# Moving the projections to the first half of the recurrent chain, and the long convolution beside its second half

## The chip, the cores and the metric

The kernel runs on one core of one Trainium2 chip. The metric is the device time of one execution in microseconds (us); the time before is the median of three runs.

## The reference

The model has two layers over 1024 latent tokens and 256 context tokens of width 1024. A layer normalises its tokens and multiplies them with one input projection, whose columns feed four groups of heads; each group's output is gated, the four are concatenated, multiplied with an output projection and added to the stream:

```
h   = rms_norm(x) * (1 + scale) + shift
z   = h @ w_in                     # 29 blocks of 128 columns
A   = hyena(z_hy)                  # two long two-sided convolutions, via a DFT
B   = rwkv7(z_rw)                  # both directions, a chain over blocks of 128 tokens
C   = window_attention(z_wa)       # +-128 tokens, context, a sink
D   = dense_attention(z_fa)        # all tokens and context
x   = x + gate * (concat(A,B,C,D * silu gates) @ w_out)
```

Layer 0 works on latent and context tokens, layer 1 (the last) needs only the latent output.

## The kernel before, in words

The program is written as straight code; a scheduler places every instruction on its engine by a simulated time line. Code that stands earlier has precedence, and work that stands later fills the gaps as far as its data and its memory are there. Memory comes from pools, and each pool lies on one of two sides of SBUF, as on a stack: the left side (the default) or the right side (`tc.using_default_side(R)`). A pool that is opened after another was closed on the same side takes its place, and each of its tiles waits until the tiles that lay there are done.

`program` goes through these stages in each layer:

- The normalised input as two operands (`hhi` and `hlo`, 80 KB a partition, left side) and `Proj` on top of it (left). `rw` makes the recurrent columns, two gate blocks follow (`PACE['pre']`), then `attn` makes queries, keys and values.
- `Rwkv.phase_a` (right side): `stage_a` for ten blocks of 128 tokens, and `solve` after the fourth, the eighth and the tenth. The last TensorE work of a block writes the bank `p_r` (L618).
- `Rwkv.phase_b` (right side, in the place of phase A): `stage_b` for ten blocks, each followed by the chain of states (`p_ch`); after the last one the blocks that one direction had left open (`pend`) follow.
- `w.beside`: the twelve projection blocks that are left (six gate blocks, six of hyena), 24 matmuls for each of three token groups in layer 0 and of two in layer 1, all at L245. Their weights are split by ScalarE (L231) and by GpSimd (`wl`, L232). They have no order of their own: `K.mark` notes the last TensorE instruction of every block of phase A (weight 1.3) and B (1.0, the first one 4.5) and of the seven late `pend` steps (0.5), 30 in all, and `K.spread` gives each token group a point between the shares `f0` and `f1` of that sum. Its matmuls are then queued behind the last mark at or before the point (`issue_after`). Phase A reaches to 13/30 = 0.433 of the sum. 
- Then all of `Proj` and the operands are closed on the left. `hyena` (for the latent tokens) and, in layer 0, `ctx_hyena` (for the context) have their pools on the right side, in the place of phase B. `attention` has its pools on the left side, in the place of the operands: window attention first (a = 0), then dense attention (a = 1), ten blocks of 128 queries each in layer 0 and eight in layer 1; each block ends with one GpSimd instruction at L1028. `OutProj` lies on the right; in layer 0 its normalised tiles are written into operands for layer 1 on the left, which are opened after attention is closed.

In hyena a half of the channels goes through `forward` twice and `inverse` twice; `forward` loads the filter's spectrum `Kf` (L1391), and its sums of eight (`Dft.eight`, `odd`, `even`) and products run on VectorE and GpSimd beside each other. SyncE (SP) issues nearly all DMAs, in order.

The functions and lines that the text speaks of:

Of the kernel before, what the change touches and what calls it, by code (L numbers as in the profile page):

```python
# [12 lines left out]
PSUM = bass.MemoryType.PSUM  # L13
# [7 lines left out]
EPS = 1e-6  # L21
B_HY, B_HYG, B_RW, B_RWG, B_WA, B_WAG, B_FA, B_FAG = 0, 6, 8, 15, 17, 21, 23, 27
NBLK = 29
PACE = {'pre': (2, 2), 'w0': (0.0, 0.0), 'wt': (3.5, 3.5), 'f0': (0.3, 0.3), 'f1': (0.7, 0.7)}


def consts():
# [126 lines left out]
def operands(hp):  # L154
    return [hp.tile([128, 8, TOK], F32R, name=n) for n in ("hhi", "hlo")]
# [265 lines left out]
class Rwkv:  # L421
# [22 lines left out]
    def phase_a(w, ep, sp, pp):  # L444
# [30 lines left out]
        def stage_a(b, n):  # L475
# [138 lines left out]
            for d in range(2):  # L614
                for h in range(4):
                    for c in range(2):
                        z = half(1 - c)
                        nc.tensor.matmul(pr[half(c), d, h, :], GA[z, d, h % 2, h // 2, c, :], VS[z, h * 64:h * 64 + 64], start=True, stop=True)  # L618
            k.mark(1.3 + (PACE["w0"][l] if n == 0 else 0.0))
            cpy(AL[:, 1], pr.rearrange("p d h v -> p d (h v)"))  # L620
# [38 lines left out]
    def phase_b(w, sp, pp):  # L659
# [28 lines left out]
        def stage_b(b, n):  # L688
# [86 lines left out]
            if need_y:  # L775
# [5 lines left out]
                cpy(ST[:, 1536:1792].rearrange("p (h v) -> p h v", h=4), py)  # L781
            k.mark(1.0 + (PACE["wt"][l] if n == 0 else 0.0))
            return ST
# [286 lines left out]
class OutProj:  # L1070
# [24 lines left out]
    def bank(w, nm):  # L1095
        return w.pp.tile([128, 512], F32, tag="o", bufs=3, name=nm)
# [263 lines left out]
def hyena(k, l, kd, sp, pp):  # L1360
# [3 lines left out]
    n, p, R = L, 128, R8  # L1364
    bank = lambda nm: pp.tile([128, 512], F32, tag="b", bufs=3, name=nm)
    tile_ = lambda shape, tag, bufs=1, P=128: sp.tile([128] + shape, F32, tag=tag, bufs=bufs, name=tag)[:P]
# [20 lines left out]

    def forward(o_, hf):
        u = U[hf]
        Kf = tile_([R, 2, 128], "Kf", 2, p)  # L1390
        nc.sync.dma_start(out=Kf, in_=kd[o_, hf])  # L1391

        def tr(rs):
            ps = bank("pr").rearrange("p (r j e) -> p r j e", r=2, j=2)[:p]
            for a, r in enumerate(rs):
                for j in range(2):
                    nc.tensor.matmul(ps[:, a, j], F[:, r, j, :], u[:, r, :], start=True, stop=True)
            return ps

        W = tile_([R, 2, 128], "W", 2, p)  # L1400
        S, D = ft.tl(4, "s4"), ft.tl(4, "s4")
        ft.pair(S[:, 2:4], D[:, 2:4], tr((1, 3)), tr((5, 7)))
        ft.pair(S[:, 0:2], D[:, 0:2], tr((0, 2)), tr((4, 6)))
        ft.eight(W, S, D, False)
        t = tile_([R, 2, 128], "t", 1, p)
        h = R // 2
        for a, z, e in ((h, R, TT), (0, h, PT)):
            s = slice(a, z)
            e(t[:, s], W[:, s], Kf[:, s, 1:2, :].to_broadcast([p, z - a, 2, 128]), op=ALU.mult)
            e(W[:, s], W[:, s], Kf[:, s, 0:1, :].to_broadcast([p, z - a, 2, 128]), op=ALU.mult)  # L1410
            e(W[:, s, 0], W[:, s, 0], t[:, s, 1], op=ALU.subtract)
            e(W[:, s, 1], W[:, s, 1], t[:, s, 0], op=ALU.add)
        Z = tile_([R, 2, 128], "Z", 2, p)
        S, D = ft.tl(4, "s4"), ft.tl(4, "s4")
        TT(D[:, 2:4], W[:, 4:6], W[:, 6:8], op=ALU.subtract)
        TT(D[:, 0:2], W[:, 0:4:2], W[:, 1:4:2], op=ALU.subtract)
        PT(S[:, 0:2], W[:, 0:4:2], W[:, 1:4:2], op=ALU.add)
        PT(S[:, 2:4], W[:, 4:6], W[:, 6:8], op=ALU.add)
        ft.eight(Z, S, D, True)
        return Z  # L1420
# [32 lines left out]
    for o_ in range(2):  # L1453
        Zs = []
        for hf in range(2):
            Zs.append(forward(o_, hf))
            yield
        for hf in range(2):
            inverse(o_, hf, Zs[hf])
            yield  # L1460
# [112 lines left out]
def program(nc, tc, A, out):  # L1573
    k = K(nc, tc, A)
    hyenas = (("", hy_filters, hyena, [2, 2, 128, R8, 2, 128]), ("c", ctx_filters, ctx_hyena, [2, 128, 2, 2, 256]))
    run = lambda g: [None for _ in g]
    R = "right"
    with k.pool("cp", 1) as cp, k.pool("dp", 1, DRAM) as dp:
        setup(k, cp, dp)

        def filters(l):
            for nm, f, _, shape in hyenas[:2 if l < DEPTH - 1 else 1]:
                k.kd[l, nm] = dp.tile(shape, F32, name=f"kd{l}{nm}")
                with tc.using_default_side(R), k.pool(f"hf{l}{nm}") as sp, k.pool(f"hfp{l}{nm}", 1, PSUM) as pp:
                    run(f(k, l, k.kd[l, nm], sp, pp))

        k.kd = {}
        for l in range(DEPTH):
            last = l == DEPTH - 1
            rw = Rwkv(k, l, cp, dp)  # L1590
            with ExitStack() as es:
                if l == 0:
                    held = ExitStack()
                    with tc.using_default_side(R):
                        ap = es.enter_context(k.pool("raw"))
                    hi, lo = norm_in(k, held.enter_context(k.pool(f"hp{l}")), ap)
                filters(l)
            with held:
                with k.pool(f"pj{l}") as sp, k.pool(f"pjp{l}", 1, PSUM) as pp:
                    w = Proj(k, l, hi, lo, sp, pp)  # L1600
                    run(w.rw())
                    todo = [(g, i) for g in (1, 2, 3, "h", 0) for i in range(6 if g == "h" else 2)]
                    early = PACE["pre"][l]
                    w.beside(todo[:early])
                    if not last:
                        for a, parts in ((l, (1,)), (l + 1, (0, 1))):
                            with tc.using_default_side(R), k.pool(f"mod{a}") as rs, k.pool(f"modp{a}", 1, PSUM) as rp:
                                modulation(k, a, parts, 3, rs, rp)
                    with k.pool(f"pa{l}") as sa, k.pool(f"pap{l}", 1, PSUM) as pq:
                        run(w.attn(sa, pq))  # L1610
                    with tc.using_default_side(R), k.pool(f"re{l}") as re, k.pool(f"ra{l}") as rs, k.pool(f"rap{l}", 1, PSUM) as rp:
                        run(rw.phase_a(re, rs, rp))
                    with tc.using_default_side(R), k.pool(f"rb{l}") as rs, k.pool(f"rbp{l}", 1, PSUM) as rp:
                        run(rw.phase_b(rs, rp))
                    w.beside(todo[early:], PACE["f0"][l], PACE["f1"][l])
                k.marks = []
            with ExitStack() as es:
                at = ExitStack()
                for nm, _, f, _ in hyenas[:1 if last else 2]:
                    with tc.using_default_side(R), k.pool(f"hy{l}{nm}") as rs, k.pool(f"hyp{l}{nm}", 1, PSUM) as rp:  # L1620
                        run(f(k, l, k.kd[l, nm], rs, rp))
                sp, pp = at.enter_context(k.pool(f"at{l}")), at.enter_context(k.pool(f"atp{l}", 1, PSUM))
                with tc.using_default_side(R):
                    op = OutProj(k, l, es.enter_context(k.pool(f"op{l}")), es.enter_context(k.pool(f"opp{l}", 1, PSUM)))
                for a in range(2):
                    run(attention(k, l, a, sp, pp))
                at.close()
                if last:
                    op.tiles(range(8), out)
                else:  # L1630
                    held = ExitStack()
                    hi, lo = operands(held.enter_context(k.pool(f"hp{l + 1}")))
                    with k.pool(f"nrmp{l}", 1, PSUM) as pp:
                        op.tiles([8, 9] + list(range(8)), out, (hi, lo, pp))
# [26 lines left out]
```

## Time and profile before

| | us |
|---|---|
| median of three runs | 2611.66 (2608.37 to 2614.43) |
| the profiled execution | 2599.59 |
| its span | 2597.8 |
| TensorE matmul busy | 2294.4 (88% of the span) |
| VectorE busy | 1696.6 (65%) |
| ScalarE busy | 1105.8 (43%) |
| GpSimd busy | 1012.8 (39%) |
| granted TensorE clock, mean | 0.913 |

Busy shares are means over the span. Matmuls are pipelined and their ends are modelled, so that a busy TensorE is not TensorE at its peak. The granted clock is a share of 2.4 GHz, 0.5 being 1.2 GHz.

### The profile page before, as it was taken

How to read it: one execution, taken by the hardware profiler on the slowest of the kernel's cores; microseconds unless marked ns; L12 is line 12 of the kernel's file. 1: busy time of each engine (PE TensorE's matmuls, PEld its weight loads, DVE VectorE, ACT ScalarE, POOL GpSimd, SP SyncE). 2: the span in 40 equal slices, each digit the busy share in tenths (PEclk: the TensorE clock that was granted, in tenths of full speed). 3: DMA queues.
4: the chain of work that ended last, by engine and by line, in shares of the span. 5: the costliest groups of instructions: out<-in, count | busy, mean ns of one | idle time of the engine just before them, and what ended most of it. 6: DMA issues, size and time to landing. Idle time of an engine off the chain costs nothing. (4 is left out here: it accounts for less than half of the span.)

```text
span 2597.8 us, 45285 instructions
## 1 busy us (share of the span) xinstructions
PE 2294.4 (88%) x16864; PEld 1873.1 (72%) x16864; DVE 1696.6 (65%) x3669; ACT 1105.8 (43%) x2622; POOL 1012.8 (39%) x1279
## 2 busy tenths in 40 slices
PE   7799999889999898878897997998999979887698
PEld 3688678667788786656686887976777868666466
DVE  6985247698734567797344776677886345779933
ACT  5422224444232576545444221344443347654451
POOL 1631223366622114464322233324676211336542
PEclk9899998779999899889998998987799989998799
DMA  7223773544364746411444124335445475641152
GB/s 261 93 90 112 247 219 116 151 143 147 107 228 141 196 150 159 165 33 70 139 129 133 72 74 152 114 112 147 136 133 161 161 201 171 163 154 49 42 162 98
DMA packets 288696, 359.12 MB, mean 138 GB/s; under 512 B 108007, under 2 KB 229910, under 8 KB 283100
## 3 DMA queue, kind: packets, MB, share of 16 engines
q1 hardware_dynamic: 264008, 271.04, 33.6%
q0 software_dynamic: 11232, 70.78, 7.9%
q10 hardware_dynamic: 13236, 14.40, 2.0%
q8 instruction: 133, 2.18, 0.3%
q14 instruction: 87, 0.71, 0.1%
HBM read 227.31 MB, written 128.84 MB: 137 GB/s over the span
## 5 line engine op out<-in xcount | busy, mean ns | idle before, releaser
L232 POOL TENSOR_TENSOR wl<-wr,wh 128x1024 fp32r<-128x1024 f32 x58 | 145.1, 2507 | 276.2 <-ACT wh L231 198.9
L986 DVE TENSOR_REDUCE st<-S 128x1 f32<-128x512 f32 (+1 forms) x320 | 173.2, 557 | 102.0 <-PE S L982 57.7
L245 PE MATMUL acc<-hhi,wh 128*128 128x512 f32 (+1 forms) x896 | 222.8, 387 | 15.0 <-ACT wh L231 10.0
L981 PE MATMUL S<-kp,qs 128*128 128x256 f32 (+2 forms) x384 | 151.0, 402 | 85.5 <-ACT P L996 64.1
L245 PE MATMUL acc<-hlo,wh 128*128 128x512 f32 (+1 forms) x896 | 215.8, 376 | 2.6 <-DVE hlo L211 2.6
L996 ACT ACTIVATE P<-S,st 128x512 f32<-128x512 f32 (+1 forms) x320 | 184.2, 588 | 79.4 <-DVE st L989 74.2
L245 PE MATMUL acc<-hhi,wl 128*128 128x512 f32 (+1 forms) x896 | 216.0, 376 | 0.0
L245 PEld LDWEIGHTS acc<-hhi,wh 128*128 128x128 f32 x896 | 160.8, 198 | 50.4 <-ACT wh L231 11.9
L1012 PE MATMUL pt<-ident,P 128*128 128x128 f32 x976 | 169.0, 296 | 29.8 <-ACT PT L952 23.3
L245 PEld LDWEIGHTS acc<-hlo,wh 128*128 128x128 f32 x896 | 157.8, 193 | 33.5 <-DVE hlo L211 3.1
L952 ACT COPY PT<-pt 128x512 f32<-128x512 f32 (+2 forms) x298 | 141.0, 497 | 88.0 <-PE pt L1012 86.2
L245 PEld LDWEIGHTS acc<-hhi,wl 128*128 128x128 f32 x896 | 155.1, 191 | 31.7 <-issue 3.2
L1012 PEld LDWEIGHTS pt<-ident,P 128*128 128x128 f32 x976 | 122.1, 150 | 61.6 <-ACT PT L952 30.7
L981 PEld LDWEIGHTS S<-kp,qs 128*128 128x128 f32 x384 | 78.5, 205 | 114.9 <-ACT P L996 78.0
L1022 PE MATMUL O<-PT,V 128*64 128x256 f32 x976 | 132.1, 388 | 3.3 <-ACT PT L952 2.7
L982 PE MATMUL S<-kp,qs 128*128 128x256 f32 (+2 forms) x384 | 126.7, 342 | 3.7 <-DMA kp<-qk_d 3.7
L1022 PEld LDWEIGHTS O<-PT,V 128*64 128x64 f32 x976 | 70.6, 138 | 45.6 <-issue 6.7
L340 ACT ACTIVATE qx<-acc 128x256 f32<-128x256 f32 x76 | 29.2, 385 | 171.6 <-PE acc L335 152.5
L231 ACT ACTIVATE wh<-wr 128x1024 fp32r<-128x1024 f32 x58 | 60.7, 1057 | 94.3 <-PE acc L245 75.0
L589 PEld LDWEIGHTS p_g<-AR,BKT 64*128 64x128 f32 x640 | 77.0, 221 | 30.9 <-issue 6.8
L335 PE MATMUL acc<-wh,hhi 128*128 128x256 f32 x608 | 95.0, 298 | 4.5 <-ACT qx L340 2.5
L335 PE MATMUL acc<-wl,hhi 128*128 128x256 f32 x608 | 92.4, 290 | 6.4 <-POOL wl L232 6.4
(404 smaller groups left out, 5918.7 us busy)
## 6 DMA issues: line engine op xcount, KB each, us to landing
IN<-in_d POOLq DMA_DIRECT2D x18, 2048.0 KB, 9.4
wr<-in_w_in POOLq DMA_DIRECT2D x58, 512.0 KB, 4.6
mw<-in_mod_w SPq DMA_DIRECT2D x48, 512.0 KB
in_d<-BK SPq DMA_DIRECT2D x20, 512.0 KB
in_d<-AL SPq DMA_DIRECT2D x20, 512.0 KB
kp<-qk_d SPq DMA_DIRECT2D x32, 320.0 KB
qk_d<-qo SPq DMA_DIRECT2D x72, 128.0 KB
in_d<-GG SPq DMA_DIRECT2D x18, 512.0 KB
```

The lines of the kernel that those rows point to most:

```text
L231: w.k.nc.scalar.activation(h, r, AF.Copy)
L232: w.k.nc.gpsimd.tensor_tensor(lw, r, h.bitcast(F32), op=ALU.subtract)
L245: nc.tensor.matmul(ps[:, :n], a[:, kc * 128:(kc + 1) * 128], b[:, kc, t0:t0 + n], start=(i == 0 and kc == 0), stop=(i == 2 and kc == 7))
L335: nc.tensor.matmul(ps[:, :256], x_[:, kc, t * 128:(t + 1) * 128], w_[:, kc, :], start=(n == 0 and kc == 0), stop=(n == 2 and kc == 7))
L589: nc.tensor.matmul(pg[:, hp, c], BKT[q, hp, c], AR[q, :, hp, half(c)], start=True, stop=True)
L952: nc.any.tensor_copy(o, i)
L981: nc.tensor.matmul(ps[:, w0:w0 + w], qs[:, hd % 2, hd // 2], kp[kv][0][:, t0:t0 + w], start=True, stop=False)
L982: nc.tensor.matmul(ps[:, w0:w0 + w], qs[:, hd % 2, hd // 2], kp[kv][1][:, t0:t0 + w], start=False, stop=not masks)
L986: TR(ng[:, i:i + 1], ps[:, :w0], axis=AX.X, op=ALU.max, negate=True)
L996: nc.scalar.activation(P[:, :w], ps[:, :w], AF.Exp, bias=gm, accum_out=den[:, i:i + 1])
L1012: nc.tensor.transpose(pt[:, i, :], P[:, i * 128:(i + 1) * 128], k.ident)
L1022: nc.tensor.matmul(O[kv * 64:kv * 64 + 64, 0], V[:, t, kv * 64:kv * 64 + 64], PTs[kv][:, i], start=(i == 0), stop=(i == nt - 1))
```

## The change

Three lines change. The point from which the twelve projection blocks are spread goes from 0.3 to 0.0 of the marks' sum, and the last point from 0.7 to 0.5. Hyena's pools are opened on the left side, in the place of the operands; attention, opened later on the same side, then lies in the place of hyena. `Kf` has one buffer instead of two.

```
-PACE = {'pre': (2, 2), 'w0': (0.0, 0.0), 'wt': (3.5, 3.5), 'f0': (0.3, 0.3), 'f1': (0.7, 0.7)}
+PACE = {'pre': (2, 2), 'w0': (0.0, 0.0), 'wt': (3.5, 3.5), 'f0': (0.0, 0.0), 'f1': (0.5, 0.5)}
...
     def forward(o_, hf):
         u = U[hf]
-        Kf = tile_([R, 2, 128], "Kf", 2, p)
+        Kf = tile_([R, 2, 128], "Kf", 1, p)
         nc.sync.dma_start(out=Kf, in_=kd[o_, hf])
...
                 for nm, _, f, _ in hyenas[:1 if last else 2]:
-                    with tc.using_default_side(R), k.pool(f"hy{l}{nm}") as rs, k.pool(f"hyp{l}{nm}", 1, PSUM) as rp:
+                    with k.pool(f"hy{l}{nm}") as rs, k.pool(f"hyp{l}{nm}", 1, PSUM) as rp:
                         run(f(k, l, k.kd[l, nm], rs, rp))
```

## Rows read from the trace of the kernel before

**Rows 1.** Stretches: start:end, length, busy us (instructions) of PE, PEld, DVE, ACT, POOL; clock, DMA, GB/s.

```profile
432.00:568.00 136.00, 113.29 (x692) 87.45 (x693) 105.68 (x197) 64.49 (x136) 69.26 (x106) 0.69 0.50 144
568.00:722.00 154.00, 147.09 (x910) 120.43 (x908) 120.46 (x231) 58.41 (x108) 90.14 (x174) 0.98 0.47 144
...
1050.00:1225.00 175.00, 135.64 (x870) 106.79 (x871) 150.64 (x244) 84.48 (x230) 97.55 (x73) 0.86 0.23 79
...
1283.00:1400.00 117.00, 114.35 (x531) 95.03 (x531) 47.22 (x62) 51.64 (x113) 34.05 (x31) 0.98 0.33 104
1717.00:1826.00 109.00, 97.97 (x579) 74.06 (x579) 79.14 (x146) 53.12 (x113) 42.71 (x54) 0.68 0.46 134
...
2300.00:2461.00 161.00, 113.86 (x748) 91.92 (x748) 144.84 (x216) 67.36 (x182) 99.92 (x71) 0.82 0.19 69
...
2510.00:2592.00 82.00, 76.50 (x338) 63.01 (x336) 34.63 (x39) 15.58 (x22) 26.20 (x25) 0.98 0.33 112
```

**Rows 2.** The projections' matmuls (L245) alone in three stretches: PE, PEld; clock, DMA, GB/s.

```profile
568.00:722.00 154.00, 109.40 (x506) 85.01 (x506) 0.98 0.47 144
722.00:835.00 113.00, 72.24 (x342) 56.19 (x342) 1.00 0.48 161
...
1826.00:2010.00 184.00, 113.05 (x432) 83.46 (x432) 0.90 0.47 142
```

**Rows 3.** Time line of PE: start, length; phase A's last `p_r`, the projections' last, attention's first.

```profile
669.41 0.56 PE L618 MATMUL p_r<-VV,GG 64*64 64x64 f32 x12
...
835.35 0.96 PE L245 MATMUL acc<-hhi,wl 128*128 128x512 f32 x3
...
866.45 0.55 PE L981 MATMUL S<-kp,qs 128*128 128x256 f32 x1 [7.40 <-DMA qs<-qk_d]
...
1954.20 0.56 PE L618 MATMUL p_r<-VV,GG 64*64 64x64 f32 x12
...
2089.09 0.96 PE L245 MATMUL acc<-hhi,wl 128*128 128x512 f32 x3
```

**Rows 4.** The chain of waits between layer 1's projections and its attention: start, length.

```profile
2103.42 14.20 DMA qs<-qk_d
...
2119.02 0.55 PE S L981
```

**Rows 5.** The context's hyena, its first and last instructions: ns min/median/max, first and last start.

```profile
L1531 PE MATMUL pd<-ident,zc x8: 273/273/273, 1221.2 to 1221.9; 128*128 128x128 f32 x8
...
L1560 DVE TENSOR_TENSOR gx<-pi,gx x1: 692/692/692, 1247.5 to 1247.5; 128x512 f32<-128x512 f32 x1
```

**Rows 6.** Groups by line, 1050 to 1225: attention's largest VectorE group there.

```profile
L986 DVE TENSOR_REDUCE st<-S 128x1 f32<-128x512 f32 (+1 forms) x66 | 37.6, 593 | 14.0 <-PE S L982 13.8
```

**Rows 7.** Time lines of VectorE and GpSimd within a solve: start, length.

```profile
678.89 2.42 DVE L646 TENSOR_TENSOR tmp<-Lx,X 64x81 f32<-64x81 f32 x1
681.35 0.24 DVE L647 TENSOR_TENSOR X<-X,tmp 64x81 f32<-64x81 f32 x1
...
678.83 2.40 POOL L232 TENSOR_TENSOR wl<-wr,wh 128x1024 fp32r<-128x1024 f32 x1
```

**Rows 8.** Time line of GpSimd: the ends of query blocks in layer 1.

```profile
2160.04 0.72 POOL L1028 TENSOR_TENSOR om<-om,gt 128x256 f32<-128x256 f32 x1 [1.06 <-ACT om L1027]
...
2256.12 0.73 POOL L1028 TENSOR_TENSOR om<-om,gt 128x256 f32<-128x256 f32 x1
...
2283.13 0.74 POOL L1028 TENSOR_TENSOR om<-om,gt 128x256 f32<-128x256 f32 x1 [4.07 <-ACT om L1027]
...
2303.70 0.73 POOL L1028 TENSOR_TENSOR om<-om,gt 128x256 f32<-128x256 f32 x1 [12.77 <-ACT om L1027]
...
2453.97 1.17 POOL L1028 TENSOR_TENSOR om<-om,gt 128x256 f32<-128x256 f32 x1
```

**Rows 9.** Stretch 2283 to 2304, columns as in the first group.

```profile
2283.00:2304.00 21.00, 18.51 (x134) 12.40 (x134) 11.65 (x36) 15.24 (x44) 4.09 (x6) 1.00 0.60 210
```

**Rows 10.** Waits of the SyncE queue, 1030 to 1290: us in total, times, longest.

```profile
SPq L1391 <- DVE W L1410: 44.1, 2, 26.8
```

More of the change, by code (lines that the diff above doesn't have):

```diff
@@ L23 @@
 NBLK = 29
-PACE = {'pre': (2, 2), 'w0': (0.0, 0.0), 'wt': (3.5, 3.5), 'f0': (0.3, 0.3), 'f1': (0.7, 0.7)}
+PACE = {'pre': (2, 2), 'w0': (0.0, 0.0), 'wt': (3.5, 3.5), 'f0': (0.0, 0.0), 'f1': (0.5, 0.5)}
 def consts():
@@ L1389, in forward @@
         u = U[hf]
-        Kf = tile_([R, 2, 128], "Kf", 2, p)
+        Kf = tile_([R, 2, 128], "Kf", 1, p)
         nc.sync.dma_start(out=Kf, in_=kd[o_, hf])
@@ L1619, in program @@
                 for nm, _, f, _ in hyenas[:1 if last else 2]:
-                    with tc.using_default_side(R), k.pool(f"hy{l}{nm}") as rs, k.pool(f"hyp{l}{nm}", 1, PSUM) as rp:
+                    with k.pool(f"hy{l}{nm}") as rs, k.pool(f"hyp{l}{nm}", 1, PSUM) as rp:
                         run(f(k, l, k.kd[l, nm], rs, rp))
```

## The prediction

> **What bounds the kernel now.** I read the kernel by stages, since the mean shares hide what each stage waits for. Phase A runs alone on TensorE at first: in 432 to 568 TensorE is busy for 113 of 136 us, but at a granted clock of 0.69, so with pauses in which the clock fell to its lower level, and VectorE is busy for 106 us [rows 1]. From 568 the projections run beside phase A and go on into phase B until 835 [rows 1 to 3]; the reader is to see the clock rise to 0.98, and VectorE at 120 of 154 us. From 866 window attention fills the gaps of phase B. Then hyena runs beside dense attention, and there TensorE is poorly used again: 136 of 175 us at clock 0.86 in layer 0, 114 of 161 at 0.82 in layer 1, with VectorE at 151 and 145 us, that is 86 to 90% [rows 1]. The output projection closes the layer with TensorE full, 117 and 82 us [rows 1]. So each layer has two stretches bound by VectorE (phase A, hyena), and the change gives both of them new companions: phase A gets all projections, hyena gets phase B instead of attention, attention gets the output projection.
>
> **The change, part by part.** All times are those of the profiled execution (2599.6 us; its span of 2597.8 and 1.8 around it).
>
> *Projections from 0.0 to 0.5 of the marks.* The same 864 and 576 matmuls run, so nothing is added; they move. Phase A's blocks get longer where they had TensorE to themselves. The first stretch of each layer in [rows 1] is cut where its last block's `p_r` is done: six blocks in layer 0, 136/6 = 22.7 us each, five in layer 1, 109/5 = 21.8. The next ones, beside projections, take (670.0 - 568)/4 = 25.5 and (1954.8 - 1826)/5 = 25.8 [rows 1, 3]. The difference is 2.8 and 4.0; I take the dearer for both, 6 x 4 = 24 us in layer 0, 5 x 4 = 20 in layer 1. The last `p_r` comes at 670 + 24 = 694 and 1955 + 20 = 1975. Bounds: 0, if projections only fill waits (the clock of 0.69 speaks for it), and twice that, 48 and 40, since the splits of weights hit the solves too: beside one split of 2.40 us on GpSimd a VectorE step of the solve took 2.42 us, its neighbour 0.24 [rows 7]. I take the value between, because it is what blocks of phase A beside projections show.
>
> Phase A ends at mark 0.433 of 0.5, so 0.067/0.5 = 13% of the projections' work comes behind it. That work is 109.4 + 72.2 + 3 = 185 us in layer 0 and, by count, 113 x 576/432 = 151 us in layer 1 [rows 2]: 25 and 20 us. The projections end at 719 and 1995 instead of 836 and 2090.
>
> *Hyena on the left.* It must wait for the operands' place, that is for the last projection, and then for its loads; attention needed 866.5 - 836.3 = 30 us for that, 2119.0 - 2090.1 = 29 us in layer 1, of which one load took 14.2 us [rows 3, 4]. Hyena's first loads are fewer and I take 15 us (bounds 5 and 30). It then runs beside phase B and the end of the last solve. Beside attention it took 175 and 161 us with VectorE 86 to 90% busy [rows 1]. No row shows it beside phase B. From below: of the 151 us of VectorE, at least 38 are attention's reductions [rows 6], so hyena's own work is about 110 us, and it can't take less than 110/0.86 = 128. From above: phase B stands earlier in the code and has precedence, and its waits on SyncE stand in one line with hyena's; 240 us would be a third more than now. I take 187 and 173 us, the present length and 12 us for phase B's first claim, because phase B, like attention, leaves VectorE the larger part of the time. `Kf` with one buffer: its load has waited for the products twice already, up to 26.8 us [rows 10], so I give the lost buffer 0 to 4 us in each of the four passes and take it as within the 12. The context's hyena follows, 1248.2 - 1221.0 = 27 us [rows 5]. Hyena ends at 719 + 15 + 187 + 27 = 948 and 1995 + 15 + 173 = 2183; the last solve, itself some 20 us later, still holds VectorE at hyena's start in layer 1, which I put at 6 us: 2189.
>
> *Attention follows there.* It waits for hyena's tiles, then loads: first scores at 948 + 30 = 978 and 2189 + 29 = 2218, instead of 866 and 2119. It starts 112 and 99 us later, and must make up for it. A window block beside phase B takes (2256.1 - 2160.0)/7 = 13.7 us; a dense block without hyena (2283 to 2303.7) 20.6 us, beside hyena (2303.7 to 2454.0)/5 = 30.1 us [rows 8]. For the context's four blocks I estimate 9 us each, below the window block's, as they have fewer keys. Now the dense blocks have the output projection beside them: TensorE is busy for 18.5 of 21 us there, part of it phase B's end [rows 9], so I put attention's need at 17 and let a block be stretched to 23 us. Layer 0: 4 x 9 + 8 x 13.7 + 8 x 23 = 330 us, end at 1308. Layer 1: 8 x 13.7 + 8 x 23 = 294, end at 2512. Before, attention ended at about 1283 and 2510: it does not end earlier.
>
> *Output projection.* It loses its wait for hyena's place on the right: its weights can be there as soon as phase B is done. A tile costs 117/10 = 11.7 us in layer 0 and 82/8 = 10.25 in layer 1 [rows 1]. In layer 0 the normalised tiles need attention's place on the left, and with two buffers each for `xt` and `y` I let four of the ten tiles go ahead, in the 8 x 6 = 48 us that TensorE has beside attention. Six follow: 70 us, layer end 1378 instead of 1400, 22 us gained. In layer 1 no such wait exists; 48 of the 82 us are done in the gaps, 34 follow: 2512 + 34 = 2546 instead of 2592, 46 us gained. If these gaps weren't used, layer 0 would lose 48 us and layer 1 48, less the 16 us by which blocks then aren't stretched in each: that is the cover that this part hangs on.
>
> **Sum.** 22 + 46 = 68 us less: 2599.6 - 68 = 2532 for the profiled execution. The median of the three runs is 12.1 us above it, so 2544, which I round to 2545.
>
> **Rivals.** (1) *Hyena short.* Phase B waits mostly on its own chain, so hyena could run at its own pace, 135 us instead of 187 and 173: 52 + 38 = 90 us earlier. TensorE is then the bound behind it, and I let three quarters through: 2545 - 68 = 2477. For it: hyena's VectorE work is only about 110 us. Against it: phase B's VectorE work comes in many short pieces between its matmuls.
>
> (2) *A lock between VectorE and GpSimd.* The row: a VectorE step with two operands in SBUF took 2.42 us instead of 0.24 while GpSimd had its 2.40 us split [rows 7]. In this kernel that would act as follows: hyena's long sums on VectorE and GpSimd already take turns, and phase B brings GpSimd work of its own into that stage, where attention had one instruction of 0.73 us a block [rows 8]. If one long step of hyena loses 2.4 us in this way for each of some seven blocks of phase B beside it, each layer ends 17 us later: 2545 + 34 = 2579. The Trainium skill, SBUF — State Buffer, section "Who interferes with whom", says that a VectorE instruction with two SBUF inputs and a GpSimd instruction that reads SBUF block each other entirely; by that rule this rival holds, and the row agrees with it for the solve, while none shows it for hyena beside phase B. Against it: most of phase B's VectorE steps read PSUM.
>
> (3) *Slower: hyena becomes the end of the chain.* Attention can't start before hyena's last tile, in both layers. If hyena beside phase B takes 33 us a layer more than I took (220 and 206 us), the gain is gone; at 240 in layer 0 and as much more in layer 1 (53 us each) it is 2545 + 106 = 2651. For it: precedence of phase B, one queue on SyncE in which a waiting `Kf` or `zc` load holds up phase B's loads [rows 10], TensorE so little used that its clock falls below the 0.82 to 0.86 of now. Against it: attention, too, took a quarter of VectorE from hyena.
>
> (4) *Nothing gained.* Hyena as forecast, but the output projection doesn't get into attention's gaps: 2545 + 2 x (48 - 16) = 2609, as before.
>
> **How the numbers follow.** Forecast 0.41, rival 1 0.18, rival 2 0.09, rival 3 0.25, rival 4 0.07. The forecast's own range is 2500 to 2595 (phase A's bounds, 0 to twice, are -44 to +44). The 8-in-10 range reaches to rival 1 and half way into rival 3: 2470 to 2645. What differs by under 0.2% can't be told from no change by such runs. Faster: forecast, rivals 1 and 2, 0.68. Same: 0.07 from rival 4 and edges. Slower: 0.25.
>
> **What would show it.** Phase A's blocks at 26 to 27 us from the first on, at a clock above 0.9; the last L245 within 30 us of the last `p_r`; the first hyena transpose some 15 us behind it; hyena 160 to 200 us long, with VectorE above 80%; first scores near 978 and 2218; dense blocks of 21 to 24 us, with `ops` matmuls between them. The forecast is wrong if hyena is over 220 us long, if `ops` starts only after attention, or if phase A's blocks go beyond 32 us.

## The result, and the profile after

The changed kernel took 2678.56 us (median of four runs, 2676.49 to 2680.37); the kernel before, beside it on the same chip, 2610.01 (2598.94 to 2614.43). The ratio is 1.0269, with a 95% interval of 1.0236 to 1.0302: about 70 us slower. The forecast was 2545, its range 2470 to 2645. It failed in sign and in size.

The profiled execution has a span of 2678.2 us, 80.4 more than before. (The medians lie 69 us apart; the trace of the kernel before is from one of its shorter executions, 2599.6, that of the changed kernel from its longest, 2680.4.) The first rows are the engine totals of its page, section 1.

```profile
span 2678.2 us, 45232 instructions
...
PE 2268.4 (85%) x16864; PEld 1858.2 (69%) x16864; DVE 1726.8 (64%) x3706; ACT 1097.8 (41%) x2585; POOL 1016.8 (38%) x1279
```

The same 16864 matmuls ran, and TensorE's busy time even fell by 26 us (2294.4 before). So all of the lost time, and more, is time in which TensorE stood idle. The next rows are stretches of the changed kernel, with the columns of [rows 1]: layer 0 from phase A to the output projection, then layer 1 from the end of its projections.

```profile
446.00:710.00 264.00, 251.21 (x1713) 202.67 (x1713) 211.22 (x366) 128.01 (x246) 154.22 (x231) 0.97 0.51 152
...
743.00:764.00 21.00, 0.10 (x1) 0.13 (x2) 2.83 (x9) 0.24 (x1) 5.37 (x11) 0.59 0.92 364
...
776.00:964.00 188.00, 132.62 (x1825) 124.56 (x1825) 157.40 (x239) 47.77 (x122) 121.52 (x122) 0.82 0.41 140
964.00:1009.00 45.00, 37.74 (x444) 33.62 (x442) 18.02 (x43) 9.48 (x24) 8.52 (x13) 0.89 0.55 200
1009.00:1035.00 26.00, 9.42 (x216) 7.90 (x208) 10.92 (x41) 1.92 (x5) 4.13 (x5) 0.64 1.03 221
...
1174.00:1387.00 213.00, 194.39 (x1124) 143.04 (x1123) 94.26 (x233) 113.98 (x307) 12.89 (x15) 0.95 0.13 39
...
1387.00:1458.00 71.00, 57.95 (x274) 48.14 (x275) 31.98 (x45) 41.18 (x96) 26.16 (x22) 0.90 0.37 130
...
2062.00:2074.00 12.00, 0.00 (x0) 0.00 (x0) 11.03 (x31) 0.18 (x1) 9.65 (x31) 0.60 0.65 242
2074.00:2260.00 186.00, 119.28 (x1445) 112.07 (x1446) 159.28 (x218) 45.29 (x113) 117.18 (x128) 0.79 0.46 159
...
2412.00:2633.00 221.00, 196.54 (x1154) 145.22 (x1151) 103.34 (x249) 128.28 (x329) 43.68 (x35) 0.98 0.26 86
...
2633.00:2667.00 34.00, 24.89 (x96) 20.00 (x96) 6.42 (x9) 3.26 (x4) 4.86 (x5) 0.80 0.22 70
```

Phase A is the stage that got what the change wants: its 264 us are at clock 0.97 with TensorE 95% busy, where the first 136 us of it stood at 0.69 [rows 1]. Then comes a hole in each layer behind the projections' end: 743 to 764, with no engine above 26%, and 2062 to 2074, without one matmul, where VectorE is at the last solve. Hyena beside phase B (776 to 964, 2074 to 2260) has TensorE busy for 71 and 64% of the time, at a clock of 0.8; beside attention it had been 78 and 71% [rows 1]. Then attention waits for its own loads (1009 to 1035), and runs with the output projection at 89 to 91%.

TensorE's idle time (length of a stretch less TensorE's busy time in it), stage by stage, worked out from such rows of both kernels:

| TensorE idle, us | layer 0 before | after | layer 1 before | after |
|---|---|---|---|---|
| phase A to the projections' end | 30 | 13 | 28 | 17 |
| changes of stage | 13 | 22 + 17 | 15 | 37 |
| phase B and its companion | 12 (attention) | 63 (hyena) | 11 (attention) | 54 (hyena) |
| the rest of attention and its companions | 49 (hyena) | 43 (output projection) | 53 | 36 |
| output projection alone | 1 | 13 | 1 | 9 |
| sum | 105 | 170 | 108 | 153 |

(The first row begins with phase A, at 433 and 1719 before and 446 and 1789 after; the fifth ends with the last `ops`, before at 1398 and 2587. The changes of stage are 836 to 866 and 2090 to 2119 before; 743 to 776, 1009 to 1035 and 2062 to 2111 after. In layer 1 attention's loads fall beside phase B, 2260 to 2294, and are in that row.) The idle time grew by 110 us in the two layers, and TensorE's busy time fell by 26: that is the 80 us within a few. Summed over both layers, phase A gives 28 us back, the changes of stage cost 48 more, and the three rows of phase B, attention and the output projection 91 more. The row to read is phase B's. Beside attention it left 12 us idle, beside hyena 63. Before, one poorly filled pair (hyena with attention) stood beside two well filled ones; now the poor pair is hyena with phase B, the well filled pair of phase B and attention is gone, and the output projection, which filled TensorE to 98% by itself [rows 1], stands in a pair at 90%.

The hole after the projections, seen on TensorE's time line (start, length; in brackets the idle time before and what ended it):

```profile
741.75 0.86 PE L245 MATMUL acc<-hhi,wl 128*128 128x512 f32 x3
763.90 5.00 PE L1381 MATMUL pd<-ident,zc 128*128 128x128 f32 x28 [21.29 <-DMA zc<-hy_d]
...
776.10 1.17 PE L733 MATMUL p_t<-IN,Y 128*128 128x128 f32 x9
```

and in the DMA view of 743 to 765 (totals; then issues, KB each):

```profile
DMA packets 1155, 8.07 MB, mean 367 GB/s; under 512 B 112, under 2 KB 112, under 8 KB 771
...
IN<-in_d POOLq DMA_DIRECT2D x2, 2048.0 KB, 15.4
zc<-hy_d SPq DMA_DIRECT2D x2, 1024.0 KB
F<-in_fw SPq DMA_DIRECT2D x1, 1024.0 KB
```

Phase A and the projections now end together, so phase B's first blocks (`IN`) and hyena's inputs (`zc`, `F`) are fetched in the same 21 us: 8.07 MB at 367 GB/s, with the DMA engines 92% busy. Before, the two stages changed over at different times, phase B's first loads beside projections and attention's beside phase B.

### The profile page after: what moved, and what is told of

It reads as the page before. It is cut to its first block, busy times and chain, and to the rows that moved or that the text cites. A ratio compares the mean times of both kernels' runs of the same rounds, so it can differ in the third digit from the quotient of the medians.

```text
span 2678.2 us, 45232 instructions
## 1 busy us (share of the span) xinstructions
PE 2268.4 (85%) x16864; PEld 1858.2 (69%) x16864; DVE 1726.8 (64%) x3706; ACT 1097.8 (41%) x2585; POOL 1016.8 (38%) x1279
## 5 line engine op out<-in xcount | busy, mean ns | idle before, releaser
L245 PE MATMUL acc<-hhi,wh 128*128 128x512 f32 (+1 forms) x896 | 226.4, 389 | 13.0 <-ACT wh L231 8.9
L245 PE MATMUL acc<-hhi,wl 128*128 128x512 f32 (+1 forms) x896 | 228.8, 386 | 0.0
L245 PE MATMUL acc<-hlo,wh 128*128 128x512 f32 (+1 forms) x896 | 222.4, 382 | 2.9 <-DVE hlo L211 2.9
L245 PEld LDWEIGHTS acc<-hhi,wh 128*128 128x128 f32 x896 | 159.7, 198 | 48.2 <-ACT wh L231 10.8
L245 PEld LDWEIGHTS acc<-hlo,wh 128*128 128x128 f32 x896 | 158.7, 195 | 36.2 <-issue 4.8
L245 PEld LDWEIGHTS acc<-hhi,wl 128*128 128x128 f32 x896 | 157.3, 193 | 37.0 <-issue 10.1
L1012 PE MATMUL pt<-ident,P 128*128 128x128 f32 x976 | 161.3, 287 | 20.2 <-ACT PT L952 9.9
L981 PE MATMUL S<-kp,qs 128*128 128x256 f32 (+2 forms) x384 | 141.7, 378 | 42.7 <-ACT P L996 27.4
L1012 PEld LDWEIGHTS pt<-ident,P 128*128 128x128 f32 x976 | 115.0, 145 | 56.1 <-ACT PT L952 19.2
L952 ACT COPY PT<-pt 128x512 f32<-128x512 f32 (+2 forms) x252 | 116.8, 491 | 76.3 <-PE pt L1012 73.7
L1028 POOL TENSOR_TENSOR om<-om,gt 128x256 f32<-128x256 f32 x36 | 26.4, 735 | 317.2 <-ACT om L1027 317.2
L982 PE MATMUL S<-kp,qs 128*128 128x256 f32 (+2 forms) x384 | 121.5, 329 | 4.7 <-DMA kp<-qk_d 4.7
L1123 POOL TENSOR_TENSOR y<-y,xt 128x512 f32<-128x512 f32 x36 | 49.3, 1375 | 173.1 <-DVE y L1122 78.8
L1121 PE MATMUL ops<-woh,mh 128*128 128x512 f32 x288 | 85.4, 442 | 23.4 <-ACT mh L1112 23.4
```

Source lines behind the costliest of these rows:

```text
L245: nc.tensor.matmul(ps[:, :n], a[:, kc * 128:(kc + 1) * 128], b[:, kc, t0:t0 + n], start=(i == 0 and kc == 0), stop=(i == 2 and kc == 7))
L952: nc.any.tensor_copy(o, i)
L981: nc.tensor.matmul(ps[:, w0:w0 + w], qs[:, hd % 2, hd // 2], kp[kv][0][:, t0:t0 + w], start=True, stop=False)
L982: nc.tensor.matmul(ps[:, w0:w0 + w], qs[:, hd % 2, hd // 2], kp[kv][1][:, t0:t0 + w], start=False, stop=not masks)
L1012: nc.tensor.transpose(pt[:, i, :], P[:, i * 128:(i + 1) * 128], k.ident)
L1121: nc.tensor.matmul(ps, a[:, kc, :], b[:, kc, s], start=(n == 0 and kc == 0), stop=(n == 2 and kc == 7))
```

## The experiments

All ratios are to the kernel before, run on the same chip. Three questions were asked: which part of the change costs, whether VectorE's and GpSimd's sharing is the cost, and whether hyena's length decides the time.

**The spread alone (E1) and the place alone (E2).** E1 is the kernel before with the new spread:

```
-... 'f0': (0.3, 0.3), 'f1': (0.7, 0.7)}
+... 'f0': (0.0, 0.0), 'f1': (0.5, 0.5)}
```

> One part alone: projections spread from 0.0 to 0.5 of the marks, hyena on the right side with two Kf buffers, as before. Theory G (hyena, put before attention on the left, is what costs: attention starts at 1035 instead of 866 and nothing gives that back): here attention may follow the projections' end near 742, so the time is about that of before or below, 2540 to 2620 us. Theory P (the new spread costs: phase A's start 13 us later, its blocks 27 us longer in layer 0, and as much in layer 1): 2660 us or more, like the changed kernel's 2679.

Measured: 2640.90 us, 1.0150 [1.0127, 1.0173], between both theories: the spread alone costs 1.5%, with hyena still on the right, and attention free to start early. Two stretches of its trace show where TensorE stands idle:

```profile
745.00:789.00 44.00, 7.09 (x29) 5.34 (x28) 10.97 (x55) 8.22 (x32) 7.42 (x18) 0.53 0.96 250
...
2412.00:2509.00 97.00, 32.30 (x186) 29.85 (x184) 84.20 (x77) 2.35 (x4) 67.70 (x48) 0.61 0.05 19
```

The hole after the projections is there too, 44 us of it, since attention's and phase B's loads now come together. Attention starts early (780 against 866) and so is done early; in layer 1 hyena's last 97 us then have nothing beside them, with TensorE at a third.

E2 is the changed kernel with the old spread (0.3 to 0.7), so that hyena is on the left and has to wait for projections that end late:

> The other part alone: hyena on the left side with one Kf buffer, projections from 0.3 to 0.7 as before. Theory G: the projections end near 836, hyena follows, attention starts near 1100 in layer 0, some 70 us later than in the changed kernel, in each layer: 2780 to 2850 us. Theory P: without the new spread the loss goes, 2590 to 2630 us.

Measured: 2776.70 us, 1.0667 [1.0634, 1.0700], as Theory G has it and 3 us below its range. Projections end at 840 and 2197, hyena runs 853 to 1040 and 2209 to 2392, and attention starts at 1108 and 2420. That hyena gates attention on the left is shown here; the new spread is what keeps that from costing 6.7%. The parts don't add: 1.5 and 6.7% alone, 2.7% together.

**Hyena first in line (E3).** The changed kernel with hyena's code ahead of phase B's, so that hyena has precedence. (`f1` becomes 1.1538 here: the marks are now those of phase A alone, 13 of 30, and 1.1538 x 13 is the same point as 0.5 x 30.)

```
-                    with ... k.pool(f"rb{l}") as rs, ...: run(rw.phase_b(rs, rp))
...
                     run(f(k, l, k.kd[l, nm], rs, rp))      # hyena
+                with ... k.pool(f"rb{l}") as rs, ...: run(rw.phase_b(rs, rp))
```

> The changed kernel with hyena written ahead of phase B in the code, so that hyena has precedence where both are ready (the projections' points are the same marks of phase A as in the changed kernel). If phase B's precedence is what stretched hyena (200 us from its first transpose to its last store in layer 0, 156 before), hyena is at 130 to 160 us, attention starts 40 to 60 us earlier in each layer and the time is 2570 to 2610 us. If hyena is held by its own work or by the lock between VectorE and GpSimd, it stays at 180 us or more and phase B is only pushed back: 2660 to 2700 us.

Measured: 2666.56 us, 1.0257 [1.0223, 1.0290], whose interval overlaps that of the change: the time is the second theory's, and hyena's length lies between both. Hyena shrank from 198 to 174 us and from 186 to 174, and attention began at 1011 and 2264 instead of 1035 and 2294. But from there to the layer's end it took 434 and 385 us instead of 423 and 373: 11 and 12 us of the lead were lost again there, where more of phase B is left over and TensorE is already 87% busy (316.44 of 362 us, 1011 to 1373). A shorter hyena is not worth its full value.

**Two `Kf` buffers (E4).** The third line of the change undone:

```
-        Kf = tile_([R, 2, 128], "Kf", 1, p)
+        Kf = tile_([R, 2, 128], "Kf", 2, p)
```

> The changed kernel with two Kf buffers again. If the single buffer costs what the prediction allowed, 0 to 4 us in each of four passes and two layers, the time is 0 to 30 us below the changed kernel's 2679 us. If Kf's load is hidden behind the other half's sums, it is within 5 us of it.

Measured: 2898.24 us, 1.1146 [1.1102, 1.1191], far from what either theory gave. The edit changes memory alone, and it takes hyena out of its place beside phase B: hyena begins at 959, after phase B's last matmul at 950, in layer 1 at 2375 after 2366. So the single buffer, which I had priced as a small loss, is what makes the overlap possible at all. The run also shows hyena with no companion: 140 us in both layers. Beside phase B it takes 198 and 186.

**The ends of the spread (E5, E8).** `f0` 0.05 (E5), and `f0` 0.05 with `f1` 0.6 (E8), in the changed kernel:

> The changed kernel with the projections' first point at 0.05 instead of 0.0, so that no group may go ahead of phase A's first block. In the changed kernel one block of projections runs ahead of phase A, whose first matmul comes 13 us later (446 instead of 433). If that delay is passed on to the end, it is won back in both layers: 10 to 13 us each, 2652 to 2660 us where the changed kernel has 2679. If it only moves work that fits in elsewhere, within 6 us of the changed kernel.

> The changed kernel with the projections from 0.05 to 0.6 of the marks: a few blocks are left when phase A's last solve runs and phase B starts. Theory H (what is lost is TensorE's idle time at the handover: no engine works from 743 to 764 while 8 MB are loaded, and phase B's first matmul is at 776 instead of 722): projections cover the handover and the time falls to 2630 to 2660 us. Theory G (hyena's start gates all that follows, and it waits for the last projection): hyena and attention start 15 to 25 us later in each layer than in the changed kernel, 2690 to 2730 us.

Measured: E5 2672.54 us, 1.0251 [1.0220, 1.0283]; E8 2667.35, 1.0249 [1.0208, 1.0290]. Both intervals overlap the change's own, so neither is told apart from it. E8 lies between its two theories: hyena starts no later in layer 0 (762), in layer 1, counted from the end of layer 0, 20 us later (636 us behind it instead of 616), and no time beyond noise is won or lost. In E5 phase A did start at 434 instead of 446, but hyena's first transpose still came at 765 (764 in the changed kernel). What the late start of phase A costs isn't told from nothing.

E5 shows something more. Its phase A and last solve end earlier, so that phase B's loads land earlier and its first matmul comes at 747 instead of 776. The hole in layer 0 is nearly filled:

```profile
746.00:765.00 19.00, 15.17 (x218) 14.21 (x219) 6.42 (x16) 7.03 (x18) 4.31 (x11) 0.91 0.97 343
```

But the idle time only moved. From the projections' end to the end of the context's hyena TensorE is idle for 81 us in E5 (746 to 1005) and for 85 in the changed kernel (743 to 1009), and the first scores come at 1033 and 1035. So in layer 0 the hole is hardly a cost of its own: until attention may start, TensorE has only the matmuls of phase B and hyena, and what they don't fill stays idle, at the start of the stretch or later.

**VectorE and GpSimd (E6, E7).** E6 moves phase B's copies (L724, L727) from GpSimd to ScalarE; E7 puts all of hyena's elementwise work on VectorE:

```
-    TT, PT = nc.vector.tensor_tensor, nc.gpsimd.tensor_tensor
+    TT = PT = nc.vector.tensor_tensor
...
     ft = Dft(k, sp)
+    ft.PT = TT
```

> The changed kernel with phase B's copies of V (five a block, 0.4 us each, L724 and L727) on ScalarE instead of GpSimd. If GpSimd work of phase B blocks hyena's sums (rival 2 of the prediction), hyena (200 us in layer 0, 187 in layer 1) gets 10 to 20 us shorter in each layer and the time is 2640 to 2660 us. If it is VectorE's own work that phase B adds, hyena stays at 190 to 200 us and the time within 8 us of the changed kernel's 2679.

> The changed kernel with all of hyena's GpSimd work (52 products and sums and its part of the sums of eight) on VectorE. If the two engines mostly wait for each other in that stage, hyena does not get longer, 160 to 200 us in layer 0, and the time is 2640 to 2690 us. If they run beside each other and VectorE is simply full (87 to 99% in most of that stage), hyena grows by the moved work, some 45 us a layer, and the time is 2740 to 2780 us.

Measured: E6 2656.18 us, 1.0190 [1.0151, 1.0229]; E7 2627.27, 1.0078 [1.0055, 1.0101]. Hyena shrank to 172 and 167 us in E6, as its first theory had it or more, and to 157 and 148 in E7, whose time lies below both of its ranges. (E7's trace is of an execution of 2609.25 us.) The groups of hyena's products in layer 0 (mean ns after the comma), first in the changed kernel:

```profile
L1409 DVE TENSOR_TENSOR t<-W,Kf 128x1024 f32<-128x1024 f32 x4 | 8.1, 2018 | 0.0
L1410 DVE TENSOR_TENSOR W<-W,Kf 128x1024 f32<-128x1024 f32 x4 | 7.9, 1970 | 0.1
...
L1409 POOL TENSOR_TENSOR t<-W,Kf 128x1024 f32<-128x1024 f32 x4 | 12.6, 3153 | 0.2
L1410 POOL TENSOR_TENSOR W<-W,Kf 128x1024 f32<-128x1024 f32 x4 | 9.7, 2432 | 0.1
```

and in E7, where its line numbers are one higher:

```profile
L1410 DVE TENSOR_TENSOR t<-W,Kf 128x1024 f32<-128x1024 f32 x8 | 9.7, 1230 | 0.0
L1411 DVE TENSOR_TENSOR W<-W,Kf 128x1024 f32<-128x1024 f32 x8 | 9.7, 1219 | 0.0
```

VectorE does eight products in 9.7 us by itself; for four of them beside GpSimd it needed 8.1, and GpSimd 12.6 for the other four. Neighbours in the changed kernel's time lines, VectorE's and then GpSimd's, show how:

```profile
788.92 1.23 DVE L1410 TENSOR_TENSOR W<-W,Kf 128x1024 f32<-128x1024 f32 x1
...
836.93 1.21 DVE L1409 TENSOR_TENSOR t<-W,Kf 128x1024 f32<-128x1024 f32 x1
838.17 3.26 DVE L1410 TENSOR_TENSOR W<-W,Kf 128x1024 f32<-128x1024 f32 x1
```

```profile
789.00 3.35 POOL L1409 TENSOR_TENSOR t<-W,Kf 128x1024 f32<-128x1024 f32 x1
...
795.24 2.34 POOL L1410 TENSOR_TENSOR W<-W,Kf 128x1024 f32<-128x1024 f32 x1
...
836.98 3.37 POOL L1409 TENSOR_TENSOR t<-W,Kf 128x1024 f32<-128x1024 f32 x1
```

At 788.92 VectorE came first and took 1.23 us, GpSimd's product beside it 3.35; at 836.93 it was first again. At 838.17 VectorE came in the middle of one of GpSimd's and took 3.26. The first engine keeps the other waiting. I call this the lock. The Trainium skill, SBUF — State Buffer, section "Who interferes with whom", says so of a VectorE instruction with two SBUF inputs and a GpSimd instruction that reads SBUF, and that the order of issue decides which one blocks; the trace agrees. Over the whole program E7 shows it in the totals:

```profile
PE 2251.8 (86%) x16864; PEld 1841.9 (71%) x16864; DVE 1700.5 (65%) x3842; ACT 1094.2 (42%) x2581; POOL 850.1 (33%) x1147
```

GpSimd gave up 167 us of work (1016.8 to 850.1), VectorE took it over, and VectorE's own busy time fell by 26 us (1726.8 to 1700.5). That fall is the lock's: VectorE did more and was busy for less. E7's gain in time has a second part, though, which no run takes alone: GpSimd's shortest product took 2.34 us (at 795.24), twice VectorE's 1.22, so the moved half also gets the faster engine.

Two more rows tell whose GpSimd work holds VectorE up. In E4, with no phase B beside hyena, its products on VectorE took 2.71 and 2.47 us in the mean, longer than beside phase B: the lock is in hyena's own sharing. And in E7, where phase B's copies stay on GpSimd and hyena's work has left it, all 32 products of both layers took VectorE 1.21 to 1.41 us, eight of them with a copy beside them. So E6's gain doesn't show that the copies block VectorE. That they kept GpSimd from its half of hyena's work (32 of them, 0.53 us each in the mean, in layer 0) fits too, and no run separates the two.

**The same edits in the old order (E9, E10), and together (E11).** E9 is the kernel before with E7's edit, E10 adds E6's, E11 is the changed kernel with both and `f0` 0.05.

> The kernel before (old order, old spread) with hyena's GpSimd work on VectorE. In the changed kernel the same edit took hyena from 198 to 157 us in layer 0 and 45 us off the time. If GpSimd and VectorE block each other beside attention as well, hyena there falls from 156 to 125 to 140 us, the output projection starts that much earlier, and the time is 2560 to 2590 us, below before's 2605. If the gain belongs to the stage shared with phase B alone, it is within 8 us of before or above.

> The same, with phase B's copies of V on ScalarE too. Beside attention ScalarE is busier than beside hyena (129 of 184 us in the stretch shared by phase B and attention), so the copies cost there what they free: within 8 us of the run with hyena on VectorE alone.

> The changed order with all three edits that helped or should help: hyena on VectorE, phase B's copies on ScalarE, first point at 0.05. If what is left of the loss (2627 after the first of these edits, before 2605) is hyena's stretch and phase A's late start, the time is 2580 to 2605 us. If it is the handover, at which 8 MB are loaded with no engine at work, and the later start of attention, it stays at 2605 to 2630 us.

Measured: E9 2586.59 us, 0.9932 [0.9913, 0.9951], faster than both kernels; E10 2607.28, 1.0008 [0.9991, 1.0025]; E11 2629.68, 1.0103 [1.0080, 1.0127]. E9 came as expected. In it hyena takes 138 and 140 us beside dense attention instead of 154 and 157:

```profile
1066.00:1204.00 138.00, 97.91 (x671) 81.81 (x669) 129.99 (x267) 65.68 (x175) 5.54 (x4) 0.86 0.19 65
2306.00:2446.00 140.00, 105.49 (x728) 86.76 (x726) 132.49 (x273) 68.01 (x181) 7.83 (x5) 0.87 0.18 68
```

E10 is a miss: the copies on ScalarE, worth 0.8% beside hyena's GpSimd work, cost 0.8% in the old order without it. Why they cost there no run settles; a reason that fits, and no more, is that ScalarE serves attention beside phase B in the old order. E11 lies at the upper end of its second range: the copies and the later first point add nothing to E7. One reservation holds for all steps under 1%: every edit is scheduled anew, and moves more than it names. In E9, whose edit touches hyena alone, the projections of layer 0 end at 850 instead of 836.

**The spread without the sharing (E12).** E9 with the new spread: hyena on the right, on VectorE, projections from 0.0 to 0.5.

> Before, with hyena's elementwise work on VectorE and with the change's spread of the projections (0.0 to 0.5 of the marks); hyena stays on the right, beside dense attention. With hyena on VectorE the old order stands at 0.993 of before and the changed order at 1.008; this kernel splits the remaining 1.5% into the spread and the moving of hyena. Theory S (the spread costs, hyena's new place on top of it is about neutral): the ratio stays near the 1.008 of the changed order, 1.003 to 1.012, about 2613 to 2637 us; hyena's last part again runs with nothing beside it. Theory M (the spread cost time only because hyena then ran long without attention, and a shorter hyena pays that back; the new place costs the 1.5%): 0.990 to 0.998, about 2580 to 2600 us.

Measured: 2605.72 us, 1.0010 [0.9997, 1.0023], between both theories. With it the change can be taken in steps, with and without GpSimd in hyena:

| ratio to before | hyena shared with GpSimd | hyena on VectorE |
|---|---|---|
| old spread, old place | 1.0000 | 0.9932 |
| new spread, old place | 1.0150 | 1.0010 |
| new spread, new place | 1.0269 | 1.0078 |

Read downward, the spread costs 1.5 or 0.8% and the place on top of it 1.2 or 0.7%. (The new place includes the single `Kf` buffer.) Read across, the sharing with GpSimd, lock and slower engine together, costs 0.7, 1.4 and 1.9%: the change makes it dearer by some 1.2%, out of 2.7. The rest, 1.0078/0.9932 or 1.5% (38 us), is the reordering itself, about half from the spread and half from the place.

## Why the prediction was wrong

Its own steps against the trace. In layer 1 70 us are taken off, by which its phase A starts later (1719 to 1789).

| start or end, us | layer 0 forecast | measured | layer 1 forecast | measured less 70 |
|---|---|---|---|---|
| last `p_r` | 694 | 710 | 1975 | 1972 |
| projections end | 719 | 743 | 1995 | 1992 |
| hyena starts | 734 | 764 | 2010 | 2004 |
| hyena's last matmul | 921 | 962 | 2189 | 2190 |
| hyena for the context ends | 948 | 1008 | | |
| first scores | 978 | 1035 | 2218 | 2224 |
| attention ends | 1308 | 1387 | 2512 | 2563 |
| last `ops` | 1378 | 1458 | 2546 | 2597 |

*Phase A's blocks: right.* Ten blocks in 264 us, 26.4 each, as the dearer row said. In layer 0, where TensorE was to do 13% of the projections in 25 us behind them, it took 33. What I missed is that with a first point of 0.0 the first group of projections isn't held behind any mark: it runs ahead of phase A, which starts at 446 instead of 433 and in layer 1 10 us later against the end of layer 0. E5 took that away, and its time can't be told from the changed kernel's.

*The lead of hyena: right in kind, short in place.* I took 15 us and found 21 and 12. But I priced only hyena's wait. Phase B's first matmul comes at 776, 54 us later than before (722): 33 of it since the last solve ends later (746 against 713), the rest since its loads share those 21 us, and no projections were left to cover them. This is the hole of E1 as well. E5 filled it in layer 0, and nothing was won beyond noise.

*Hyena's length: phase B's claim on it was mis-sized, and in layer 0 luck hid it.* 198 and 186 us against 187 and 173 are 11 and 13 more, well below the 220 that I had named as the point of failure. But the 175 us of layer 0 was the length of my stretch, 1050 to 1225, and not hyena's: its matmuls ran from 1052 to 1206, 154 us, and in layer 1 157. What phase B adds is 44 and 29 us, where I had put 12. The same stretch held the wait between hyena and the context's hyena, which I then counted no more: 15 us before (1206 to 1221) and 18 after (962 to 980, 6.4 us of it for the load of `zc`). The context's hyena itself took 28.5 us, as forecast. From hyena's first transpose to its end both together took 244 us in layer 0, 30 more than my 187 + 27.

*Attention follows there: the step that failed.* "I put attention's need at 17 and let a block be stretched to 23 us." In layer 1, where everything up to the first scores came within 6 us of the forecast, attention ended 51 us late against it. The window blocks took 120 us for eight, 15.0 each against 13.7; that they came near is luck, for the 13.7 was a miscount. Between 2160.0 and 2256.1 in [rows 8] six blocks end and not seven, 16.0 us each. The dense ones were far off; GpSimd's time line at L1028 has the last window block's and the last dense block's end:

```profile
2413.16 0.73 POOL L1028 TENSOR_TENSOR om<-om,gt 128x256 f32<-128x256 f32 x1 [9.49 <-ACT om L1027]
...
2632.73 0.72 POOL L1028 TENSOR_TENSOR om<-om,gt 128x256 f32<-128x256 f32 x1 [4.21 <-ACT om L1027]
```

That is 219.6/8 = 27.4 us a block, and 26.5 in layer 0 (1175 to 1387): 36 and 28 us more than 8 x 23, together 64 of the 148 us between forecast and measurement, the largest single piece. The 23 us rested on one dense block of 20.6 us. The ends that [rows 8] leaves out say that it was the shortest of its layer:

```profile
2335.66 1.17 POOL L1028 TENSOR_TENSOR om<-om,gt 128x256 f32<-128x256 f32 x1
2367.13 0.95 POOL L1028 TENSOR_TENSOR om<-om,gt 128x256 f32<-128x256 f32 x1 [0.79 <-ACT om L1027]
2412.52 0.91 POOL L1028 TENSOR_TENSOR om<-om,gt 128x256 f32<-128x256 f32 x1
...
2485.22 0.74 POOL L1028 TENSOR_TENSOR om<-om,gt 128x256 f32<-128x256 f32 x1 [0.41 <-ACT om L1027]
2509.46 0.74 POOL L1028 TENSOR_TENSOR om<-om,gt 128x256 f32<-128x256 f32 x1 [8.50 <-ACT om L1027]
```

Beside hyena four blocks end between 2303.7 and 2454.0, not five: 37.6 us each. Of the two behind hyena one took 31.3 us and the other 24.2. Their mean, 27.7, is near what the changed kernel's blocks took.

The forecast can also be read as a sum of TensorE's work. The stretch 2412 to 2633 holds 196.5 us of TensorE's work; with the 24.9 us of the last two tiles after it (2633 to 2667) that is 221 us, and my forecast for both together was 8 x 23 + 34 = 218. In layer 0 194.4 + 58.0 = 252, my forecast 8 x 23 + 70 = 254. So what I called attention with the output projection in its gaps was TensorE's bare busy time: I let every gap be filled. (I didn't work it out so; that the sums meet is chance.) Measured were 255 and 284 us, TensorE 87 and 89% busy. For one dense block with the output projection in its gaps that is 24.6 us of TensorE's work in layer 1 (196.5/8) and 24.3 in layer 0, already more than 23, and behind it 3.1 and 2.3 us of idle time, which I had put at nothing. In layer 1 the waits in this stretch end mostly on ScalarE: 8.3 us on attention's `P`, 6.5 on the output projection's `mh`. [Rows 9] had said it: 18.5 of 21 us with phase B's end beside a dense block, 88%. I read the missing 12% as room; with another companion 9 and 11% were still missing while attention ran. The group of `ops` at layer 1's end shows a further piece:

```profile
L1121 PE MATMUL ops<-woh,mh 128*128 128x512 f32 x128 | 37.0, 435 | 16.3 <-ACT mh L1112 16.3
```

The last tiles need the last dense block's output, through memory and two engines, and TensorE waits for it (8.5 us in the chain of waits, 2633.49 to 2642.03). Before, seven of the eight tiles of `ops` came behind attention, and TensorE was busy for 76.5 of 77 us there.

*Layer 0 was lost before attention, too.* Its first scores came 57 us late: 13 from phase A's start, 3 from its blocks, 8 from the projections behind them, 6 from hyena's lead, 30 from hyena and the context's hyena, less 3 in attention's wait. Attention added 22 (28 in the dense blocks, less 6 in the others).

*The output projection's share: nearly right.* Six of eight tiles went ahead in layer 1 and 34 us remained, as forecast. In layer 0 5.5 of ten went ahead (264 of 480 matmuls) instead of four, but the rest still took 71 us (70 forecast), 11 of them a wait for normalised tiles.

*The sum.* Forecast was a gain of 22 us in layer 0 and 46 in layer 1; measured were losses of 60 in layer 0 (last `ops` 1398 to 1458), 10 in the start of layer 1's phase A, and 10 from there to the last `ops` (868 to 878 us). The differences, 82 + 10 + 56, are the 148 us between 2532 and the profiled execution.

*The rivals.* The slower one (3) named the right place: attention stands behind hyena in both layers, and E2 shows what that costs when hyena is late. Its time (2651) is near, but its condition, 33 us more of hyena in each layer, came true in neither. In layer 0 hyena and the context's hyena were 30 us longer than forecast and attention 57 us late, which is its mechanism; in layer 1 attention was only 6 us late and the gain was gone all the same, because the gain behind it had been counted on dense blocks of 23 us. Rival 2 is half right. VectorE and GpSimd do lock each other (the neighbours above), but within hyena's own sharing; that phase B's GpSimd work holds up hyena's steps on VectorE, as the rival had it, no run shows, and E7's rows speak against it for the copies. E6's 26 and 19 us are near the rival's 17 a layer, by whichever way. The sharing also was in the stretches that I took from before as if they were hyena's own need (E9: 138 and 140 us). Rivals 1 and 4 are refuted by the result.

What stays open: how the 0.8 and 0.7% of spread and place divide between the changes of stage and the poorer pairs. The table of idle time says both (changes of stage 13 to 39 and 15 to 37 us, phase B's pair 12 to 63 and 11 to 54). E5 shows for layer 0 that filling the hole with phase B moves the idle time into phase B's pair; no run let hyena, on which attention waits, load earlier. Nor did a run change what stands in the dense blocks' gaps: their 24.6 and 3.1 us are read from the trace, not tested.

## What to carry to other kernels

Before stages are paired anew, write for each pair how much of TensorE it leaves idle, and sum over all pairs: a good pair that is broken up (phase B with attention, 12 us idle) can cost more than the poor one that is mended. A companion fills what the trace has shown such a pair to fill, here 88% before and 89 to 91% after, not all; a forecast that equals TensorE's busy time has no idle time in it and is a bound, not an estimate. Read a price off all blocks that the trace holds, and not off one, and take a stage's length from its own first and last instruction. And when two stages are made to change over at the same time, add their loads, but ask which of them the next stage waits for.

## What the runs showed of the hardware

GpSimd's help can be worth less than nothing. A 128x1024 product of two SBUF operands took VectorE 1.23 us by itself, and 2.0 us in the mean with GpSimd at the other half, which needed 3.15 and 2.43 for its products, 2.34 at best; taking the help away shortened hyena by 37 to 41 us in the changed kernel and by 16 in the one before, and made the best version of this study (0.9932). Not all GpSimd work weighs alike: with copies of 64x256 on GpSimd beside them (0.53 us in the mean), VectorE's products in E7 took at most 1.41 us.
